# MLP work on VectorE and ScalarE ordered by a list of pieces with needs and due times, and the next layer's first operands made in the last unit

## The chip, the cores and the metric

The kernel runs on one core of a Trainium2 chip as a single launch. The metric is the device time of that launch in microseconds (us). The kernel before takes 2238.01 us (median of three runs, 2237.26 to 2238.69). All arithmetic is in single precision: where TensorE multiplies, each operand is split into a high part (rounded to TensorE's fast format) and a low part (what the rounding left), and three of the four products are summed.

## The reference, cut to what matters

Two layers over 256 tokens of width 2048. Each layer is an attention stage (gated linear attention and stick-breaking attention side by side) and an MLP with a hidden width of 8192:

```python
def hybrid_layer(x, ...):
    h = rms_norm(x, attn_norm)
    proj = h @ w_in
    ...                                  # two groups of heads, each normalised
    x = x + mixed @ w_o
    hm = rms_norm(x, mlp_norm)
    up = square(relu(hm @ w_up))         # 256 x 8192
    return x + up @ w_down
```

The change lies in the MLP and at the seam between the first layer's MLP and the second layer's attention. The attention stage itself is as before.

## The kernel before

**Tiles.** The 256 tokens are two blocks of 128 rows. `x` stays on chip as four tiles `xb[0..3]` of 512 columns. An operand of a product is kept transposed, as eight "pairs" of 256 contraction rows with their high and low parts (class `Operand`).

**Units.** The MLP of a layer is a list of 16 units in the order q = 0 to 3, and in each q: up 0, up 1, down 0, down 1. An up unit makes 1024 of the hidden columns; a down unit adds what q's 2048 hidden rows give to 1024 columns of `x`. A unit goes through eight steps j, each with 256 x 1024 weights (1 MB, one load by the SyncE queue, line 993, five buffers in all). In five steps the product is direct: eight block products. In the three "fast" steps, j = 1, 3 and 5 (line 298), a scheme with seven block products instead of eight (Strassen's, in Winograd's form) is used, for which VectorE first sums weight blocks: `ts` (line 1137), a sum written back into the raw weights, and `t4` (both line 1014 through `add`). A block product is three matmuls of 512 columns (lines 1008, 1010, 1011), so a unit has 5 x 8 x 3 + 3 x 7 x 3 = 183 of them.

**Parts.** Weights are split into high and low in parts of at most 128 x 1024 (`parts`, line 995): ScalarE copies the high part `whi` (line 998), then VectorE subtracts to get `wlo` (line 999). A direct step has two parts (12 matmuls each), a fast one four (6, 3, 6 and 6 matmuls). There are four buffers each of `whi` and `wlo`, so a part can be made when the matmuls of the part four places back are done. The 22 parts of a unit are numbered k = 0 to 21.

**Banks.** The unit sums into eight banks of PSUM named by the scheme's products: banks 5, 7, 1 and 6 are written from k = 4 and 5 on and are final after k = 17; banks 2, 4, 3 and 8 are written from k = 0, 1 on and are final after k = 20 (2 and 4) and k = 21 (3 and 8). When banks are final, VectorE combines them (the "tail" of the unit: `sums`, then the halves `left` and `right`, with `add` on line 1014); a down unit adds them to `xb`, an up unit puts them in `y`, and ScalarE applies the ReLU with the norm's factor (line 1060).

**From up to down.** After an up unit, TensorE transposes each half of `y` (line 1094) behind parts k = 0 and k = 1 of the next unit, into banks 5, 7 and 1, 6; ScalarE squares them (line 1103), and `forms` splits them into high and low (lines 303 and 304) and for fast pairs first makes three sums on VectorE (lines 317 to 320). These four operand pairs are made behind k = 4, 10, 13 and 15 of that unit.

**What sets the order.** In the MLP the order of TensorE, VectorE and ScalarE is the order in which the program is written (`manual_schedule`, line 1210); each engine executes its own list strictly in order. The list is written with a fixed lead: a queue holds four parts whose high and low have been written down, and only then are the oldest part's products written (`LEAD`, `emit`, lines 1192 to 1227), with the tail behind k = 17, 20 and 21. Outside that block a scheduler orders the instructions.

**The seam.** After the last unit the second layer starts with transposes of `xb[0]` and `xb[1]` (16 of them, `norm_operand`, lines 688 and 689; 332 is the transpose, 350 and 352 make the high and the low part), and then the first product with `w_in` (line 425).

Of the kernel before, what the change touches and what calls it, by code (L numbers as in the profile page):

```python
# [35 lines left out]
C_SQ, C_SK, C_SV = 3088, 4112, 5136  # L36


@with_exitstack
def trunk_kernel(  # L40
# [228 lines left out]
    def inv_rms(ss, n, width):  # L269

        v, y, t, t2, rr = stat(n), stat(n), stat(n), stat(n), stat(n)
        nc.vector.tensor_scalar(v, ss, 1.0 / width, EPS, ALU.mult, ALU.add)
        nc.scalar.activation(y, v, AF.Ln)
        nc.scalar.activation(y, y, AF.Exp, scale=-0.5)
        nc.vector.tensor_tensor(t, y, y, ALU.mult)
        nc.vector.scalar_tensor_tensor(t2, t, -0.5, v, ALU.mult, ALU.mult)
        nc.vector.scalar_tensor_tensor(rr, t2, 1.5, y, ALU.add, ALU.mult)
        return rr
# [22 lines left out]
    def split(d, t):  # L301

        nc.scalar.activation(d[:, :, 0, :], t, AF.Copy)  # L303
        return lambda: nc.vector.tensor_tensor(  # L304
            d[:, :, 1, :], t, f32(d[:, :, 0, :]), ALU.subtract
        )

    def forms(op, i, t, tag):

        lows = []
        if fast(i):
            a11, a21, a12, a22 = (t[:, k, r * P : (r + 1) * P] for k in range(2) for r in range(2))
            e = tmp("t2", [P, 3, P], bufs=4)
            d = op.x[i] = tmp(tag, [P, 3, 2, P], F32R, bufs=3)
            nc.vector.tensor_tensor(e[:, 2, :], a21, a11, ALU.subtract)
            nc.vector.tensor_tensor(a21, a21, a22, ALU.subtract)
            nc.vector.tensor_tensor(e[:, 0, :], a11, a21, ALU.subtract)
            nc.vector.tensor_tensor(e[:, 1, :], a12, e[:, 0, :], ALU.subtract)  # L320
            lows.append(split(d, e))
        lows.append(split(op.pair(i), t))
        return lambda: [low() for low in lows]

    def norm_operand(op, n, key, l, sums=False, banks=None):

        for h2 in range(2):
            pt = bank(banks[h2]) if banks else ps_tile()
# [7 lines left out]
            if sums and fast(2 * n + h2):  # L336
                t = tmp("t2", [P, 2, T], bufs=4)
                for j in range(2):
                    nc.scalar.activation(
                        t[:, j, :], pt[:, j * T : (j + 1) * T], AF.Copy,  # L340
                        scale=gain(key, l, 4 * n + 2 * h2 + j),
                    )
                forms(op, 2 * n + h2, t, "sxh")()
                continue
            d = op.pair(2 * n + h2)
            for j in range(2):
                g = gain(key, l, 4 * n + 2 * h2 + j)
                src = pt[:, j * T : (j + 1) * T]
                his.append(
                    nc.scalar.activation(d[:, j, 0, :], src, AF.Copy, scale=g).ins  # L350
                )
                nc.vector.scalar_tensor_tensor(
                    d[:, j, 1, :], src, g, f32(d[:, j, 0, :]), ALU.mult, ALU.subtract
                )

# [296 lines left out]
    for l in range(DEPTH):  # L652
# [30 lines left out]
        else:  # L683
# [4 lines left out]
            for n in range(2):  # L688
                norm_operand(hT, n, "attn", l)
# [280 lines left out]
        up = {}  # L970
        rs = {}
        units = [(q, down, n2) for q in range(4) for down in range(2) for n2 in range(2)]
        raws, banks, ys = {}, {}, {}
        begun = set()
# [10 lines left out]
        def load(x):  # L985
            if x >= 8 * len(units):
                return
            if x % 5 < 2:
                r = tmp("raw2", [P, 2, 1024], bufs=2)
            else:  # L990
                r = wpool.tile([P, 2, 1024], F32, tag="raw", name=nm("raw"))
            raws[x] = r
            nc.sync.dma_start(r, weights(*divmod(x, 8)))

        def parts(r, n=2):
            hi = ppool.tile([P, 2, 512], F32R, tag="whi", name=nm("whi"), bufs=4)
# [278 lines left out]
```

## Time and profile before

| | us |
|---|---|
| median of three runs | 2238.01 |
| the profiled execution, its own time | 2237.89 |
| its span in the profile | 2236.2 |
| MLP of layer 0, first matmul to last | 702.91 |
| MLP of layer 1, first matmul to last | 702.94 |

The profiled execution took 1.7 us more than its span, for what lies before the first and after the last instruction. The MLPs of the two layers are 63% of the span. Times in a view count from the start of the span. "Idle before" stands in brackets with the instruction that ended it. A matmul's record lasts 0.39 us, but a new one can start 0.23 us after the one before, so the records overlap, and a lost fraction of a microsecond does not show as idle time in the sum of busy time; it shows in the starts. In the same way, two VectorE instructions that do not need each other overlap by a little.

### The profile page before, as it was taken

The numbers are of one execution on the slowest core, as the hardware profiler recorded it, in microseconds if no ns is written. First come the engines' busy times: TensorE is split into PE (matmuls) and PEld (weight loads), VectorE is DVE, ScalarE is ACT, GpSimd is POOL, SyncE is SP. The second block draws the span as 40 slices with busy tenths as digits, with TensorE's granted clock in tenths as the row PEclk, the third lists the DMA queues.
The fourth block names the chain that finished last, engine by engine and source line by source line (L and its number), as shares of the span: only waits on it lengthen the run. The fifth ranks groups of instructions, "written<-read, shape, count | busy, mean of one in ns | idle before, by whom it ended". The sixth has DMA issues, their size and how long they took to land.

```text
span 2236.2 us, 27047 instructions
## 1 busy us (share of the span) xinstructions
PE 2201.8 (98%) x10376; PEld 1800.9 (81%) x10376; DVE 1818.7 (81%) x2286; ACT 1246.2 (56%) x1623; POOL 38.0 (2%) x64
## 2 busy tenths in 40 slices
PE   9999999999999999999999999999999999999999
PEld 7988778777887887887888887887778778878877
DVE  5777556789989989989967775667899899899898
ACT  5555355565556466466556553555565655564563
POOL 0020000000000000000000200000000000000000
PEclk9999999999999999999999999999999999999999
DMA  6545446455555555555446544464555555555553
GB/s 227 191 154 167 151 134 243 169 183 194 189 193 183 205 205 175 206 188 188 151 153 201 173 154 150 145 233 172 183 182 216 176 200 189 190 187 199 205 174 138
DMA packets 152549, 408.96 MB, mean 183 GB/s; under 512 B 6650, under 2 KB 31810, under 8 KB 152420
## 3 DMA queue, kind: packets, MB, share of 16 engines
q1 hardware_dynamic: 152420, 407.24, 52.8%
q8 instruction: 81, 1.33, 0.2%
q14 instruction: 48, 0.39, 0.1%
HBM read 405.12 MB, written 2.10 MB: 182 GB/s over the span
## 4 chain that ended last, share of the span: by engine, by line
PE 81%; DVE 15%; issue 2%; ACT 1%; DMA 0%; SPq 0%; POOL 0%; DVEq 0%; ACTq 0%
PE acc L425 9%; PE acc L426 9%; PE acc L427 9%; DVE wlo L999 7%; PE acc L472 3%; PE acc L476 1%; DVE xb L1014 1%; ACT whi L998 1%; DVE t L1014 1%; DVE act L304 1%; DVE ts L1137 1%; DVE act L1014 1%; DVE sx L304 1%; PE ps L895 1%; PE ps L907 1%
## 5 line engine op out<-in xcount | busy, mean ns | idle before, releaser
L999 DVE TENSOR_TENSOR wlo<-raw,whi 128x1024 fp32r<-128x1024 f32 x512 | 610.4, 1220 | 96.4 <-ACT whi L998 92.9
L998 ACT ACTIVATE whi<-raw 128x1024 fp32r<-128x1024 f32 x512 | 528.8, 1054 | 185.2 <-PE acc L427 10.0
L408 DVE TENSOR_TENSOR wlo<-raw,whi 128x1024 fp32r<-128x1024 f32 (+2 forms) x274 | 317.4, 1164 | 195.0 <-ACT whi L406 193.8
L406 ACT ACTIVATE whi<-raw 128x1024 fp32r<-128x1024 f32 (+2 forms) x274 | 273.5, 1004 | 290.9 <-PE acc L427 242.7
L425 PE MATMUL acc<-whi,act 128*128 128x512 f32 (+2 forms) x960 | 368.1, 383 | 1.2 <-ACT act L350 0.9
L426 PE MATMUL acc<-wlo,act 128*128 128x512 f32 (+2 forms) x960 | 362.0, 377 | 0.4 <-DVE wlo L408 0.4
L427 PE MATMUL acc<-whi,act 128*128 128x512 f32 (+2 forms) x960 | 361.6, 377 | 0.0
L998 ACT ACTIVATE whi<-t 128x512 fp32r<-128x512 f32 x96 | 60.8, 633 | 268.7 <-DVE t L1014 143.0
L425 PEld LDWEIGHTS acc<-whi,act 128*128 128x128 f32 x960 | 180.7, 188 | 36.5 <-issue 4.1
L427 PEld LDWEIGHTS acc<-whi,act 128*128 128x128 f32 x960 | 180.5, 188 | 33.9 <-issue 0.7
L426 PEld LDWEIGHTS acc<-wlo,act 128*128 128x128 f32 x960 | 180.8, 188 | 32.0 <-DVE wlo L408 1.2
L999 DVE TENSOR_TENSOR wlo<-ts,whi 128x1024 fp32r<-128x1024 f32 x96 | 117.4, 1223 | 1.4 <-ACT whi L998 1.4
L1137 DVE TENSOR_TENSOR ts<-raw 128x1024 f32<-128x1024 f32 x96 | 116.7, 1216 | 0.0
L998 ACT ACTIVATE whi<-ts 128x1024 fp32r<-128x1024 f32 x96 | 100.4, 1046 | 0.0
L472 PE MATMUL acc<-act,whi 128*128 128x512 f32 x256 | 91.9, 402 | 0.0
L1060 ACT ACTIVATE act<-act,st 128x512 f32<-128x512 f32 x64 | 42.8, 716 | 63.8 <-DVE act L1014 63.8
L476 PE MATMUL acc<-act,wlo 128*128 128x256 f32 x256 | 71.8, 280 | 0.0
L1014 DVE TENSOR_TENSOR raw<-ts,raw 128x512 f32<-128x512 f32 x96 | 66.4, 692 | 3.3
L1014 DVE TENSOR_TENSOR t<-raw 128x512 f32<-128x512 f32 x96 | 66.4, 692 | 3.3
L999 DVE TENSOR_TENSOR wlo<-t,whi 128x512 fp32r<-128x512 f32 x96 | 65.7, 684 | 0.0
L472 PEld LDWEIGHTS acc<-act,whi 128*128 128x128 f32 x256 | 48.1, 188 | 11.1
L303 ACT ACTIVATE sx<-t 128x384 fp32r<-128x384 f32 x24 | 12.6, 526 | 73.9 <-DVE t L320 73.9
(2384 smaller groups left out, 4629.3 us busy)
## 6 DMA issues: line engine op xcount, KB each, us to landing
raw<-in_w_up_dram SPq DMA_DIRECT2D x128, 1024.0 KB, 5.1
raw<-in_w_down_dram SPq DMA_DIRECT2D x128, 1024.0 KB, 5.3
raw<-in_w_in_dram SPq DMA_DIRECT2D x84, 1024.0 KB, 5.1
raw<-in_w_o_dram SPq DMA_DIRECT2D x32, 1024.0 KB, 5.2
raw<-in_w_in_dram SPq DMA_DIRECT2D x14, 512.0 KB, 6.6
raw<-in_w_in_dram SPq DMA_DIRECT2D x8, 544.0 KB, 3.7
out_dram<-xb SPq DMA_DIRECT2D x8, 256.0 KB, 2.0
xb<-in_x_dram SPq DMA_DIRECT2D x3, 512.0 KB, 7.6
```

The costliest lines, as they stand in the source:

```text
L304: return lambda: nc.vector.tensor_tensor(d[:, :, 1, :], t, f32(d[:, :, 0, :]), ALU.subtract)
L406: newest["hi"] = nc.scalar.activation(h, r, AF.Copy).ins
L408: newest["lo"] = nc.vector.tensor_tensor(lo[:, q : q + step, :width], r, f32(h), ALU.subtract).ins
L425: nc.tensor.matmul(o, xh[:, sl], whi[:, j, :width], start=first, stop=False)
L426: nc.tensor.matmul(o, xh[:, sl], wlo[:, j, :width], start=False, stop=False)
L427: st["mm"] = nc.tensor.matmul(o, xl[:, sl], whi[:, j, :width], start=False, stop=last).ins
L472: nc.tensor.matmul(acc[:, f, :], whi[:, j, sl], op.both(k), start=(k == 0), stop=False, skip_group_check=True,)
L476: nc.tensor.matmul(acc[:, f, T:], wlo[:, j, sl], xh, start=False, stop=(k == KT - 1), skip_group_check=True,)
L998: nc.scalar.activation(hi[:, :n], r, AF.Copy)
L999: nc.vector.tensor_tensor(lo[:, :n], r, f32(hi[:, :n]), ALU.subtract)
L1014: nc.vector.tensor_tensor(dst, a, b, ALU.subtract if sub else ALU.add)
L1137: nc.vector.tensor_tensor(t13, ends, b12.unsqueeze(1).to_broadcast([P, 2, 512]), ALU.add)
```

## The change

All MLP work becomes a list of pieces (class `Plan`). A piece has an engine, a length in us written into the program, the pieces that it needs, and a function that writes its instructions. TensorE's and SyncE's pieces keep the order in which they are listed. A piece of VectorE or ScalarE gets a due time: the latest start at which the TensorE work that hangs on it would still start on time, if TensorE never waited. Then `run` plays the list through: whenever VectorE or ScalarE is free, it takes, among the pieces whose needs are met, the one due first. The order found is the order written down, and on the chip each engine follows it as it did the old one. The needs hold the ring of four parts (`whi`, `wlo`), the five weight buffers, the banks and the sums; the high and the low parts keep their order among themselves.

The number and kind of the matmuls, splits, sums and loads are as before. Beside the order, three things differ. `ts` has one buffer and not two. The three sums of a fast pair use a tile `e` of their own (two buffers) and not one of the shared `t2`. And the transposes and splits of `xb[0]` and `xb[1]` for the second layer stand in the last unit of the first layer, behind k = 0 and k = 1, in banks 5, 7 and 1, 6; the second layer's attention starts with its first product. The first unit's `residual(3)` and the transposes of `xb[3]` are pieces of the list too.

```diff
+class Plan:
+    GAP = 0.06
...
+    def run(self):
+        t = 0.0
+        for p in self.pieces:
+            if p.engine == "PE":
+                p.due = t
+                t += p.length
+        for p in reversed(self.pieces):
+            if p.engine != "PE":
+                p.due = min([u.due for u in p.users], default=t) - p.length - p.lag - self.GAP
+        line = {e: [p for p in self.pieces if p.engine == e] for e in ("PE", "SP")}
+        free = dict.fromkeys(("PE", "SP", "DVE", "ACT"), 0.0)
+        left = {p: len(p.deps) for p in self.pieces}
+        at = dict.fromkeys(self.pieces, 0.0)
+        ready = {"DVE": [], "ACT": []}
+        order, events, count = [], [], 0
+        for p in self.pieces:
+            if not p.deps:
+                events.append((0.0, count, p))
+                count += 1
+        came = set()
+        while events:
+            now, _, p = heapq.heappop(events)
+            if p is not None:
+                if p.engine in ready:
+                    heapq.heappush(ready[p.engine], (p.due, count, p))
+                else:
+                    came.add(p)
+                count += 1
+            for e in free:
+                if free[e] > now + 1e-9:
+                    continue
+                if e in ready:
+                    if not ready[e]:
+                        continue
+                    p = heapq.heappop(ready[e])[2]
+                elif line[e] and line[e][0] in came:
+                    p = line[e].pop(0)
+                else:
+                    continue
+                order.append(p)
+                free[e] = now + p.length
+                heapq.heappush(events, (free[e], count, None))
+                count += 1
+                for u in p.users:
+                    at[u] = max(
+                        at[u], free[e] + p.lag + (0.0 if u.engine == e else self.GAP)
+                    )
+                    left[u] -= 1
+                    if not left[u]:
+                        heapq.heappush(events, (at[u], count, u))
+                        count += 1
+        assert len(order) == len(self.pieces)
+        for p in order:
+            if p.fn:
+                p.fn()
+        return max(free.values())
...
+    def operand_parts(op, n, h2, key, l, place):
...
+            e.append(tmp("e", [P, 3, P], bufs=2))
...
             att_psum()
             new_kdz()
             load_gate_up(l)
-            for n in range(2):
-                norm_operand(hT, n, "attn", l)
             uv = unit(
...
+        MM, TR, V2, V1, A2, A1 = 0.227, 0.108, 1.15, 0.61, 1.0, 0.55
+        RING, RAWS = 4, 5
...
+        tail = [add("PE", 12 * MM, None) for _ in range(RING)]
+        for t in tail:
+            whi.append([t])
+            wlo.append([t])
+        x3 = add("DVE", V2, lambda: residual(3, uo), tail)
...
+        def turned(n, h2, m, op, key, ll, deps):
+            turn, high, low, _ = operand_parts(op, n, h2, key, ll, lambda: bank(m))
+            a = add("PE", 8 * TR / 2, turn, deps, free.get(m))
+            b = add("ACT", A1, high, a)
+            c = add("DVE", 1.0, low, b)
+            free[m] = [b, c]
+            return c
...
+            piece = add("SP", 2.9, fn, raws[x - RAWS] if x >= RAWS else [], lag=4.6)
+            raws.append(readers)
+            return (lambda: box[0]), piece, readers
...
+            h = add("ACT", A2 if n == 2 else A1, high, deps, whi[i - RING], last.get("h"))
+            lo = add("DVE", V2 if n == 2 else V1, low, h, wlo[i - RING], last.get("l"))
+            last.update(h=h, l=lo)
+            whi.append([lo])
+            wlo.append([])
+            readers.extend((h, lo))
+            return box, h, lo
...
+                box["13"] = tmp("ts", [P, 2, 512], bufs=1)
...
+            t13 = add("DVE", V2, first, ld, sums13[-1] if sums13 else [])
+            t2 = vector(b12, lambda: box["13"][:, 0, :], lambda: r()[:, 1, 512:], t13)
+            t4 = add("DVE", V1, fourth, t2, sums4[-1] if sums4 else [])
...
+                w = vector(dw, bk(6), dw, c, p[6], op=ALU.subtract)
+                a = vector(x12, dw, x12, w, s[0])
+                v = vector(dw, bk(7), dw, a, p[7])
+                b = vector(x21, x21, dw, v, op=ALU.subtract)
+                d = vector(x22, dw, x22, v, s[1])
+                free.update({5: s[:2], 1: [c, s[2]], 6: [w], 7: [v]})
+                box["s"] = (s[2], b, a, d)
...
+                    free[m] = [add("DVE", V1, fn, p[m], box["s"][2 * c + tt])]
+                    got += free[m]
+                x_done[2 * n2 + c] = got
...
+                    a = add("PE", 4 * TR, turn_one, box["r", h], free[m])
+                    sq = add("ACT", A1, square, a, box.get("sq"))
+                    box["sq"] = sq
+                    free[m] = [sq]
...
+                    e = sq
+                    if fast(pair):
+                        e = add("DVE", 1.25, lambda f=made: f(0), sq)
+                    b = add("ACT", A1 * (2 if fast(pair) else 1), lambda f=made: f(1), e)
+                    done[q, pair] = add(
+                        "DVE", 1.1 if fast(pair) else V1, lambda f=made: f(2), b
                     )
...
+        for u, (q, down, n2) in enumerate(units):
+            tails[u] = (down_tail if down else up_tail)(u)
+            begun, p, k = set(), {}, 0
+            for j in range(8):
+                x = 8 * u + j
+                r, ld, readers = load(x)
+                for (box, h, lo), prods in steps(x, r, ld, readers):
+                    ready = done.get((q, j) if down else ("hm", j))
+                    for m, blocks in prods:
+                        begin, end = m not in begun, j == (7 if m in (2, 4, 3, 8) else lastf)
+                        begun.add(m)
+                        p[m] = add(
+                            "PE", 3 * MM * len(blocks),
+                            lambda a=(m, blocks, box, begin, end): product(*a),
+                            h, lo, ready, free[m] if begin else [],
                         )
+                    whi[-1].append(p[m])
+                    wlo[-1].append(p[m])
+                    if u == 0 and k == 0:
+                        for h2 in range(2):
+                            done["hm", 6 + h2] = turned(
+                                3, h2, (5, 7)[h2], hm, "mlp", l, x3
+                            )
+                        rr, rr_done = norm_last()
+                    if u and k < 2 and not units[u - 1][1]:
+                        tails[u - 1][2](k)
+                    if u + 1 == len(units) and k < 2 and l + 1 < DEPTH:
+                        for h2 in range(2):
+                            turned(
+                                k, h2, ((5, 7), (1, 6))[k][h2], hT, "attn", l + 1, x_done[k]
+                            )
+                    if j == 7:
+                        tails[u][1](k % 2, p)
+                    k += 1
+                if j == lastf:
+                    tails[u][0](p)
+        if l + 1 < DEPTH:
+            sq = [
+                add("ACT", 2 * A1, lambda n=n: norm_squares(n, ssq2), x_done[n])
+                for n in range(4)
+            ]
+            st["rst"], _ = norm_end(sq, ssq2)
         with tc.manual_schedule(engines=MANUAL):
+            plan.run()
...
-        LEAD = 4
-        queue = []
-        tails = {}
-        def emit():
-            u, k, products, w = queue.pop(0)
-            if k == 0:
-                begun.clear()
-                tails[u] = (down_tail if units[u][1] else up_tail)(u), begin(u)
-            products(w)
-            (sums, left, right), extra = tails[u]
-            if k in extra:
-                extra[k]()
-            for at, fn in ((17, sums), (20, left), (21, right)):
-                if k == at:
-                    fn()
-            for x in range(4):
-                load(x)
-            for x in range(8 * len(units)):
-                load(x + 4)
-                u, j = divmod(x, 8)
-                if j == 0:
-                    count = 0
-                for i, (prepare, products) in enumerate(steps(x)):
-                    if j == 1 and i == 0:
-                        while queue[0][0] < u:
-                            emit()
-                    queue.append((u, count, products, prepare()))
-                    count += 1
-                    if x == 0 and i == 1:
-                        residual(3, uo)
-                    if len(queue) >= LEAD and (u or count >= LEAD):
-                        emit()
-            while queue:
-                emit()
-            if l + 1 < DEPTH:
-                for n in range(4):
-                    norm_squares(n, ssq2)
-                st["rst"] = norm_finish(ssq2)
```

455 lines of the change are left out of this document (255 added, 200 removed).

## Prediction

> **What bounds the kernel now.** I read the page first, then the busy time of each engine in windows that begin and end with a unit's first matmul, then the timeline around the units that are too long.
>
> ```profile
> span 2236.2 us, 27047 instructions
> PE 2201.8 (98%) x10376; PEld 1800.9 (81%) x10376; DVE 1818.7 (81%) x2286; ACT 1246.2 (56%) x1623; POOL 38.0 (2%) x64
> PE 81%; DVE 15%; issue 2%; ACT 1%; DMA 0%; SPq 0%; POOL 0%; DVEq 0%; ACTq 0%
> ```
>
> TensorE is busy nearly all the time, yet 15% of the chain that ended last runs through VectorE. What TensorE loses is seen only in the length of the units. First five units of layer 0, then both MLPs whole (columns: length; busy time and instructions of TensorE, its weight loads, VectorE, ScalarE, GpSimd; granted clock, DMA share, GB/s):
>
> ```profile
> 417.53:462.12 44.59, 43.31 (x192) 35.02 (x191) 39.61 (x48) 25.33 (x35) 0.00 (x0) 1.00 0.52 189
> 462.12:508.63 46.51, 44.77 (x201) 35.51 (x199) 40.97 (x52) 27.18 (x36) 0.00 (x0) 1.00 0.46 158
> 508.63:553.97 45.34, 44.22 (x200) 35.70 (x200) 42.80 (x53) 29.15 (x37) 0.00 (x0) 1.00 0.53 186
> 553.97:595.57 41.60, 41.60 (x184) 34.42 (x184) 39.17 (x44) 21.67 (x23) 0.00 (x0) 1.00 0.57 206
> 595.57:637.05 41.48, 41.48 (x185) 34.35 (x183) 37.61 (x41) 22.42 (x25) 0.00 (x0) 1.00 0.61 224
> ...
> 417.53:1120.44 702.91, 690.45 (x3066) 560.53 (x3064) 644.16 (x757) 408.19 (x499) 1.69 (x2) 1.00 0.53 187
> 1529.27:2232.21 702.94, 690.35 (x3065) 560.43 (x3063) 643.11 (x755) 401.55 (x483) 0.00 (x0) 1.00 0.53 186
> ```
>
> The same 183 matmuls take 41.48 us in the fifth unit (an up unit behind a down unit), 41.60 in the fourth, but 46.51 and 45.34 in the second and third, which also hold the transposes, and 44.59 in the first. The clock is full and DMA is at half its capacity throughout. A matmul starts every 0.227 us (last four below: 0.68 us for three steps), and 183 of them make 41.5: the fifth unit has no loss at all.
>
> What do the transposes cost by themselves?
>
> ```profile
> 464.62 0.39 PE L1011 MATMUL m__754_4002<-whi,act 128*128 128x512 f32 x1
> 464.85 0.60 PE L1094 MATMUL m__755_4009<-ident,act 128*128 128x128 f32 x4
> 465.28 0.60 PE L1094 MATMUL m__756_4014<-ident,act 128*128 128x128 f32 x4
> 465.64 0.48 PE L1008 MATMUL m__759_4023<-whi,act 128*128 128x512 f32 x1
> 465.95 0.40 PE L1010 MATMUL m__759_4023<-wlo,act 128*128 128x512 f32 x1
> ```
>
> From 464.62 to 465.95 are 1.33 us with two matmul steps in them: 0.88 for one half. A unit behind an up unit has two halves, 1.75, so its floor is 43.23; the first unit has one (`xb[3]`), floor 42.36. Lost are: second unit 3.28, third 2.11, fourth 0.12, first 2.23. If this comes again in every q, a layer loses 2.23 + 4 x (3.28 + 2.11 + 0.12) = 24.3 us; it does, for 702.91 less 16 x 41.48 and 17 halves of 0.88 is 24.3 too. Both layers: 48.5.
>
> Where do the 3.28 come from? Timeline of the second unit, VectorE, ScalarE and TensorE around the longest gap:
>
> ```profile
> 495.08 0.28 DVE L317 TENSOR_TENSOR t<-act 128x128 f32<-128x128 f32 x1
> 496.05 0.29 DVE L320 TENSOR_TENSOR t<-act,t 128x128 f32<-128x128 f32 x1
> 498.40 1.22 DVE L999 TENSOR_TENSOR wlo<-raw,whi 128x1024 fp32r<-128x1024 f32 x1 [2.06 <-ACT whi L998]
> 496.38 0.53 ACT L303 ACTIVATE sx<-t 128x384 fp32r<-128x384 f32 x1 [3.92 <-DVE t L320]
> 497.33 1.99 ACT L998 ACTIVATE whi<-raw 128x1024 fp32r<-128x1024 f32 x2
> 497.62 0.39 PE L1011 MATMUL m__754_4002<-whi,act 128*128 128x512 f32 x1
> 498.42 0.50 PE L1008 MATMUL m__759_4023<-whi,act 128*128 128x512 f32 x1 [0.42 <-ACT whi L998]
> 499.68 0.50 PE L1010 MATMUL m__759_4023<-wlo,act 128*128 128x512 f32 x1 [0.76 <-DVE wlo L999]
> ```
>
> ScalarE stood idle for 3.92 us behind an `sx` copy that waited for VectorE's sums, with the next `whi`, due at once, queued behind it; then VectorE stood idle 2.06 us for that `whi`; TensorE, with no part left, lost 0.57 and 1.03 us. The work was there; the written order put pieces not yet needed ahead of one that was. Over the program:
>
> ```profile
> ACT whi L998 <- DVE t L1014: 143.0, 53, 7.2
> DVE wlo L999 <- ACT whi L998: 94.3, 102, 2.1
> ACT sx L303 <- DVE t L320: 73.9, 24, 3.9
> ```
>
> **The change part by part.**
>
> *The order, second unit.* No instruction is added; the question is whether VectorE has room. It needs 40.97 us of busy time in a floor of 43.23 and has 5.5 idle today. In the fourth unit it ran 39.17 in 41.60 (idle 5.8%) at a loss of 0.12, in a fixed order. At the same idle share the second unit takes 40.97/0.942 = 43.5: gain 3.0 of 3.28. Four per layer: 12.0. Bounds: half of it (1.6 each) where new cross waits appear, 3.28 at best.
>
> *Third unit.* Here VectorE needs 42.80 of 43.23, 99%. At the fourth unit's idle share this would be 45.4, no gain; with perfect order 2.11. Against the first speaks that the tail's sums need not end with the unit: banks 5, 7, 1 and 6 are wanted only at the next unit's k = 4, and that unit has 2.4 us of VectorE idle. I take two thirds, 1.4; four per layer: 5.6.
>
> *First unit.* Its loss begins with `residual(3)`:
>
> ```profile
> 417.74 1.23 DVE L953 TENSOR_TENSOR xb<-acc,xb 128x1024 f32<-128x1024 f32 x1 [3.12 <-PE acc L427]
> 418.88 1.22 DVE L1137 TENSOR_TENSOR ts<-raw 128x1024 f32<-128x1024 f32 x1
> ```
>
> VectorE waited 3.12 us for the last product of the stage before, with the first `ts` behind it. The list lets `ts` go ahead; 1.1 us of the queue is off, and the splits of `xb[3]`, now due by banks 5 and 7, share the rest. I take 1.7 of 2.23; bounds 0 and 2.23.
>
> Per layer 12.0 + 5.6 + 1.7 = 19.3; two layers 38.6.
>
> *Loads.* 128 a layer as before on SyncE's queue, each behind the four to seven readers of the buffer five loads back, as now; cost nothing, hidden by DMA at 0.46 to 0.61 of its time. If a load were late by 1 us it would first hit `ts`, then k = 3 of a fast step.
>
> *One `ts` buffer.* The next `ts` sum now waits until both readers of the last are done. Between one fast step's third part and the next's second, TensorE has 6 + 6 + 12 + 12 + 6 matmuls, 9.5 us. In it VectorE must do four `wlo` of 1.14, then the chain `ts`, sum, `t4`, split. The rows' durations for one chain and for instructions that need each other:
>
> ```profile
> 545.76 0.68 DVE L1014 TENSOR_TENSOR xb<-m__863_4477,xb 128x512 f32<-128x512 f32 x1
> 546.36 0.68 DVE L1014 TENSOR_TENSOR t<-m__864_4481,t 128x512 f32<-128x512 f32 x1
> 547.07 0.69 DVE L1014 TENSOR_TENSOR xb<-t,xb 128x512 f32<-128x512 f32 x1
> 549.73 3.49 DVE L999 TENSOR_TENSOR wlo<-raw,whi 128x1024 fp32r<-128x1024 f32 x3
> ```
>
> Three `wlo` take 3.49, so (3.49 - 1.22)/2 = 1.14 a piece; the 512-wide sums 0.60, or 0.71 behind one they need. Four `wlo` and the chain: 4.5 + 1.2 + 0.7 + 0.7 + 0.7 = 7.8 of 9.5. Room of 1.7: nothing, unless a fast pair's `forms` fall in the same stretch (four sums, 1.3 us from 495.08 on, and two splits of at most 0.6 each: up to 2.5).
>
> An instruction that needs nothing of the one before thus starts 0.085 us before that one's record ends. [...]
>
> *The seam.*
>
> ```profile
> 1119.53 0.39 PE L1011 MATMUL m__1814_8970<-whi,act 128*128 128x512 f32 x1
> ...
> 1120.21 0.39 PE L1011 MATMUL m__1814_8970<-whi,act 128*128 128x512 f32 x1
> 1120.44 0.60 PE L332 MATMUL ps<-ident,xb 128*128 128x128 f32 x4
> 1122.13 1.54 PE L332 MATMUL ps<-ident,xb 128*128 128x128 f32 x12 [1.09 <-DVE xb L1014]
> 1123.42 0.48 PE L425 MATMUL acc<-whi,act 128*128 128x512 f32 x1
> ```
>
> From the last MLP matmul to the first of attention are 3.21 us. Taken off: all but one step, 2.98. Put back: two halves of transposes in the last unit, 1.75. Rest 1.23. But eight splits each on ScalarE and VectorE move with them:
>
> ```profile
> L352 DVE SCALAR_TENSOR_TENSOR act<-ps,gcol_a,act 128x256 fp32r<-128x256 f32 x32 | 14.3, 479 | 2.9 <-ACT act L350 2.7
> ```
>
> On VectorE 14.3/32 x 8 = 3.6 us, which bring the last unit, by the fourth's 39.17, to 42.8 of 43.23, as tight as the third; with that unit's remainder of 0.7 the seam gives 0.5. The transposes' new wait is met: `xb[0]` is final in the unit before, and `xb[1]` two sums (0.68 each) after its last product, while its transposes stand behind two parts, 5.4 us. What stands behind them on TensorE, k = 1 and 2, would wait if not; k = 4 and 5 wait for the splits to free the banks, two to four parts later. Bounds -1.2 (the wait for the last `xb` sum moves to attention's first product) and +1.2.
>
> Sum: 38.6 + 0.5 = 39.1 off the profiled execution's own 2237.89 (its median is 0.1 higher, which is no difference here): 2198.8, forecast **2199**. All floors met: 2237.9 - 48.5 - 1.2 = 2188.
>
> **The rivals.** *A, half the gain.* VectorE becomes the bound in second and third units: the order is computed from fixed lengths and executed in order, so that a piece that is late by a few tenths holds those behind it. The second unit gains 1.6, the third and the first nothing: 8 x 1.6 = 13, 2225; with half of the third's and the first's loss besides, 8 x 2.7 + 2.2 = 24, 2214. For it: 99% in the third unit. Against: 94% ran freely in the fourth.
>
> *B, slower.* The single `ts` buffer: `forms` fall into the 9.5 us stretch, and `t4` is late at k = 3 of fast steps. Their 2.5 us less the 1.7 of room are at most 0.8 a fast step. If the order makes all 96 fast steps of the program pay, the units that are clean today too, it decides from 0.5 us a step on (48 against the 49 won); at 0.6 it is 2237.9 - 49 + 58 = 2247. Against: clean units have no `forms`.
>
> *C, nothing changes.* The same waits come back in another place, 2234 to 2242. Against: the new list knows the pieces that blocked.
>
> *D, no overlap on VectorE.* If each instruction held VectorE for its whole record, as those that need each other do, the second unit would need up to 40.97 + 52 x 0.085 = 45.4 us and gain 1.1, the third nothing: 8 x 1.1 + 2 x 1.7 + 0.5 = 12.7, 2225. Against: 1.14 for 1.22, and the third unit's 53 instructions would need 47.3 us and take 45.34. [...]
>
> **How the numbers follow.** Forecast (2188 to 2209) 0.68; A 0.22; B 0.04; C 0.04; D 0.02. Faster by over 0.2% (what a measurement of this kernel can tell from no change, 4.5 us): forecast, A, D and a quarter of C, 0.93; same 0.02 (half of C); slower 0.05 (B and the rest of C). The range: lower end 2188, no unit can go under its floor; upper end into A until two tenths are out, 2214.
>
> **What would show it.** Right: second units at 43.2 to 43.8, third at 43.2 to 44.2, first at 42.4 to 43.2; "ACT sx from DVE t" and "ACT whi from DVE t" mostly gone; the seam's first product 0.3 to 0.5 us behind the last MLP matmul. Wrong: units at 41.5 today that grow past 42, waits of TensorE on `wlo` from `t4` or `ts`, an idle VectorE in second units again, or a wait for `xb` ahead of attention's first product.

## The result and the profile after

The changed kernel takes 2199.91 us (median of four runs, 2199.17 to 2201.5), the kernel before, on the same chip, 2237.98: a ratio of 0.9831, 95% interval 0.9814 to 0.9848, or 38.1 us less. 39.1 were forecast off the profiled execution. The interval lies below 1, so it is faster, by 1.7%. The profiled execution of after took 2201.5 us, its span 2199.8; between the two profiled executions the difference is 36.4.

The page of after: span, busy time of the engines, and the shares of the chain that ended last.

```profile
span 2199.8 us, 27163 instructions
PE 2187.7 (99%) x10376; PEld 1806.0 (82%) x10376; DVE 1790.0 (81%) x2286; ACT 1259.7 (57%) x1623; POOL 38.0 (2%) x64
PE 90%; DVE 7%; issue 1%; ACT 1%; DMA 0%; SPq 0%; POOL 0%; ACTq 0%
```

The count of instructions on TensorE, VectorE, ScalarE and GpSimd is the same. VectorE's share of the chain has halved, from 15 to 7%, and its busy time has fallen by 28.7 us, which nothing in the prediction had.

The same windows as before, first matmul of a unit to first matmul of the next: first five units of layer 0, its last unit, and the two MLPs.

```profile
418.26:461.26 43.00, 42.68 (x192) 35.11 (x191) 39.29 (x50) 26.33 (x36) 0.00 (x0) 1.00 0.57 188
461.26:505.38 44.12, 43.70 (x200) 35.86 (x199) 41.04 (x54) 29.37 (x38) 0.00 (x0) 1.00 0.58 191
505.38:548.68 43.30, 43.30 (x201) 36.02 (x199) 39.60 (x49) 27.60 (x34) 0.00 (x0) 1.00 0.57 192
548.68:590.40 41.72, 41.72 (x185) 34.28 (x183) 38.21 (x44) 22.00 (x23) 0.00 (x0) 1.00 0.61 202
590.40:632.08 41.68, 41.68 (x185) 34.28 (x183) 38.20 (x44) 23.48 (x26) 0.00 (x0) 1.00 0.63 205
1061.22:1105.53 44.31, 43.90 (x200) 35.70 (x199) 41.27 (x52) 27.33 (x41) 0.30 (x1) 1.00 0.42 133
418.26:1105.53 687.27, 684.95 (x3081) 563.94 (x3080) 632.38 (x764) 419.20 (x507) 1.69 (x2) 1.00 0.58 192
1511.25:2195.81 684.56, 682.71 (x3065) 562.33 (x3063) 627.76 (x754) 409.35 (x483) 0.00 (x0) 1.00 0.58 191
```

The first unit went from 44.59 to 43.00, the second from 46.51 to 44.12, the third from 45.34 to 43.30, its floor; the fourth and fifth grew by 0.12 and 0.20. Layer 1's MLP is 18.4 shorter. Layer 0's is 15.6 shorter although its last unit now holds the transposes for the next layer. From the last MLP matmul of layer 0 to the first of layer 1's MLP (1105.30 to 1511.25) are 405.95 us, against 409.06 (1120.21 to 1529.27): 3.1 less. The MLP of layer 0 begins 0.7 later, which is put down here to the attention stage before it, not to the change (in the runs below, with that stage the same, the MLP begins anywhere from 415.8 to 418.3). 18.4 + 15.6 + 3.1 - 0.7 = 36.4.

The groups of waits of after (total us, count, longest):

```profile
DVE wlo L1179 <- ACT whi L1175: 106.1, 92, 1.5
ACT whi L1175 <- DVE t L1098: 60.7, 35, 5.1
ACT act L1344 <- DVE act L1098: 25.4, 32, 1.1
```

ScalarE's wait for `t` is 60.7 instead of 143.0, and that of the `sx` copies, 73.9 before, is gone.

What is left in a second unit, in the timeline of after:

```profile
480.26 2.01 ACT L1175 ACTIVATE whi<-raw 128x1024 fp32r<-128x1024 f32 x2 [0.24 <-PE m__764_4027 L1260]
480.82 1.22 DVE L1179 TENSOR_TENSOR wlo<-raw,whi 128x1024 fp32r<-128x1024 f32 x1
481.95 1.21 DVE L1098 TENSOR_TENSOR ts<-raw 128x1024 f32<-128x1024 f32 x1
483.09 1.21 DVE L1179 TENSOR_TENSOR wlo<-raw,whi 128x1024 fp32r<-128x1024 f32 x1
483.55 0.39 PE L1258 MATMUL m__756_3993<-whi,act 128*128 128x512 f32 x1
...
484.36 0.50 PE L1259 MATMUL m__756_3993<-wlo,act 128*128 128x512 f32 x1 [0.42 <-DVE wlo L1179]
```

The second of the two `whi` ends at 482.27, 0.3 us after VectorE took up a `ts` that nobody needed yet; its `wlo`, the urgent one, starts at 483.09. TensorE's two starts are 0.81 apart instead of 0.23. The list takes what is due first among the pieces that are ready, and it takes something whenever anything is ready.

The seam in the timeline of after:

```profile
1105.30 0.39 PE L1260 MATMUL m__1825_8996<-whi,act 128*128 128x512 f32 x1
1105.53 0.39 PE L549 MATMUL acc<-whi,act 128*128 128x512 f32 x1
```

The next layer's first product follows one matmul step behind.

### The profile page after: what moved, and what is told of

Same layout as the page of the kernel before. It is cut to its first block, busy times and chain, and to the rows that moved or that the text cites. A ratio compares the mean times of both kernels' runs of the same rounds, so it can differ in the third digit from the quotient of the medians.

```text
span 2199.8 us, 27163 instructions
## 1 busy us (share of the span) xinstructions
PE 2187.7 (99%) x10376; PEld 1806.0 (82%) x10376; DVE 1790.0 (81%) x2286; ACT 1259.7 (57%) x1623; POOL 38.0 (2%) x64
## 4 chain that ended last, share of the span: by engine, by line
PE 90%; DVE 7%; issue 1%; ACT 1%; DMA 0%; SPq 0%; POOL 0%; ACTq 0%
PE acc L549 9%; PE acc L551 9%; PE acc L550 9%; DVE wlo L1179 3%; PE acc L596 3%; PE acc L600 1%; DVE ts L1098 1%; DVE act L426 1%; PE ps L1017 1%; PE ps L1029 1%; ACT whi L1175 1%; PE ps L441 0%; PE ps L976 0%; PE ps L712 0%; DVE sx L426 0%
## 5 line engine op out<-in xcount | busy, mean ns | idle before, releaser
L1179 DVE TENSOR_TENSOR wlo<-raw,whi 128x1024 fp32r<-128x1024 f32 x512 | 618.5, 1217 | 56.8 <-ACT whi L1175 52.9
L1175 ACT ACTIVATE whi<-t 128x512 fp32r<-128x512 f32 x96 | 60.6, 631 | 122.2 <-DVE t L1098 60.7
L600 PEld LDWEIGHTS acc<-act,wlo 128*128 128x128 f32 x256 | 48.4, 189 | 0.1
```

The lines of the kernel that those rows point to most:

```text
L600: nc.tensor.matmul(acc[:, f, T:], wlo[:, j, sl], xh, start=False, stop=(k == KT - 1), skip_group_check=True,)
L1175: nc.scalar.activation(box["h"][:, :n], src(), AF.Copy)
L1179: nc.vector.tensor_tensor(box["l"][:, :n], src(), f32(box["h"][:, :n]), ALU.subtract)
```

## Experiments

The theory to be tested: the time was lost to the order and not to VectorE's capacity; the due times won it back; what is left comes from starting an unneeded piece just ahead of an urgent one. Against it stand rival A (VectorE itself is full, or an order from fixed lengths is held up by pieces that are late) and rival B (the single `ts`).

**1. Without due times: the piece that is ready first goes first.**

```diff
-                    heapq.heappush(ready[p.engine], (p.due, count, p))
+                    heapq.heappush(ready[p.engine], (0.0, count, p))
```

> The changed kernel, but a free VectorE or ScalarE takes the piece whose needs were met first; the due times are not used, all else is as changed. Theory (the due times carry the gain: urgent parts go ahead of sums that can wait): 10 to 30 us of the 38 come back, 2210 to 2230, with waits of TensorE on wlo in all kinds of units. Rival (what cost time was only that an engine stood behind a piece whose needs were not met; any order that takes ready pieces alone does away with it): 2198 to 2204.

Measured: 2250.78 us, ratio to before 1.0057 (1.0042 to 1.0072), slower than the hand-written order and beyond the 2210 to 2230 expected. Fourth unit, and a row of TensorE's timeline in it:

```profile
551.24:594.43 43.19, 41.84 (x184) 34.20 (x183) 38.41 (x44) 22.12 (x23) 0.00 (x0) 1.00 0.58 197
```
```profile
554.11 0.50 PE L1258 MATMUL m__920_4754<-whi,act 128*128 128x512 f32 x1 [1.35 <-DVE xb L1098]
```

VectorE does the same work (38.41 us; 38.21 in after), but a `xb` sum that frees a bank comes late, and a unit that was clean loses 1.6. Everything else of the change is in this kernel too (the pieces, the single `ts`, the tile `e`, the moved seam), so none of that makes it faster by itself: the due times carry more than the whole gain.

A small part of the 12.8 us is the clock. In one unit of each layer TensorE stands idle for 2.21 us behind a `wlo`, and then the granted clock is half for 3.41 us (the first of the two):

```profile
828.97 0.80 PE L1259 MATMUL m__1352_6792<-wlo,act 128*128 128x512 f32 x1 [2.21 <-DVE wlo L1179]
828.93:832.34 3.41, 3.37 (x8) 2.70 (x9) 3.41 (x5) 0.00 (x0) 0.00 (x0) 0.50 0.11 17
```

Those two units take 47.3 us where the same units elsewhere in the run take 45.8, so 3.0 us in all.

**2. Due times, and a look ahead.** While the list is played through, a ready piece is passed over if its length would make a more urgent one late whose start is already known.

```diff
-                    p = heapq.heappop(ready[e])[2]
+                    pick = None
+                    for item in sorted(ready[e]):
+                        c = item[2]
+                        if not any(
+                            s.due < c.due and now + c.length > max(at[s], s.due + late)
+                            for s in soon[e]
+                        ):
+                            pick = item
+                            break
+                    if pick is None:
+                        continue
```

(`soon` holds the pieces of an engine whose needs have all been started, `late` is how far TensorE is behind its due times.)

> The changed kernel, but a free engine leaves a ready piece, and waits if it must, where that piece would make a more urgent one late whose start is already known. Theory (what is left in second units, 0.87 us, and in fourth and fifth, 0.2 each, comes from a ts or weight sum begun some tenths of a us before a wlo that was due could start): second units 43.3 to 43.6, the others within 0.1 of their floors, 2188 to 2194 in all. Rival (VectorE is simply full in second units): they stay at 44.0, 2198 to 2202, or grow because VectorE now waits.

Measured: 2189.58 us, ratio 0.9782 (0.9768 to 0.9797), faster than both kernels. Second, third and fourth unit:

```profile
459.02:502.36 43.34, 43.34 (x201) 35.93 (x199) 41.11 (x54) 29.41 (x38) 0.00 (x0) 1.00 0.60 194
502.36:545.65 43.29, 43.29 (x201) 36.02 (x199) 39.59 (x49) 27.59 (x34) 0.00 (x0) 1.00 0.58 191
545.65:587.16 41.51, 41.51 (x185) 34.35 (x183) 38.22 (x44) 22.00 (x23) 0.00 (x0) 1.00 0.60 203
```

With the same work on VectorE (41.11; 41.04 in after) the second unit falls from 44.12 to 43.34. All units but layer 0's last are within 0.15 us of the floors that the prediction took from the transposes' rows. Layer 0's last unit, which holds the moved transposes, takes 43.77. So the rest of after's loss, in the second units as in the fourth and fifth, was the early start of unneeded pieces.

**3. The seam alone, put back**, once in after and once in the version with the look ahead.

```diff
             load_gate_up(l)
+            for n in range(2):
+                norm_operand(hT, n, "attn", l)
...
-                    if u + 1 == len(units) and k < 2 and l + 1 < DEPTH:
-                        for h2 in range(2):
-                            turned(
-                                k, h2, ((5, 7), (1, 6))[k][h2], hT, "attn", l + 1, x_done[k]
-                            )
```

> The changed kernel, but the transposes and splits of xb[0] and xb[1] are back at the start of the second layer. Theory (the seam is worth about 0.5 us, as predicted: 3.0 off the gap, 2.6 on the last unit): 2200 to 2201.5, the gap from the last MLP matmul to attention's first product near 3.2 again, the last unit at 41.7. Rival (the moved splits cost the last unit nothing that counts, so the seam is worth 1.2 or more): 2201.2 to 2203; or it is worth less than nothing: below 2199.5.

> The kernel that looks ahead (e2), with the seam as before the change. Theory (with the last unit at its floor the seam is worth 2.98 less 1.75 or a little less): 1.0 to 1.5 us more than e2, 2190.5 to 2191.2; last unit 41.5, gap 3.2. Rival (the last unit was never the place; the seam's worth is the same 0.5 or less): 2189.2 to 2190.2.

Measured: 2201.27 us, ratio 0.9837 (0.9822 to 0.9851), and 2191.85, ratio 0.9791 (0.9777 to 0.9806): 1.4 and 2.3 above the versions with the moved seam, but the intervals overlap, and the second was measured on another chip than its version with the moved seam (the kernel before takes 0.55 longer there). The traces tell more. From the last MLP matmul to layer 1's MLP are 410.21 us instead of 405.95 with the seam back in after, and the last unit is 41.7 instead of 44.31: the move is worth 4.26 - 2.6 = 1.7 there. With the look ahead it is 1.5 by the same reckoning (409.79 - 406.04 outside the MLP, 43.77 - 41.51 in the last unit). So in after the traces give the rival's 1.2 or more and not the theory's 0.5, though not for the rival's reason: the moved splits do cost the last unit 2.6, and what differs is the old seam. Its gap to attention's first product is 2.84 us, where 3.2 was expected. With the look ahead the traces give the 1.0 to 1.5 of the theory, though the time itself, 2191.85, lies above its 2191.2. One row of the first of the two shows what the old seam has beside that gap:

```profile
1106.65 0.50 PE L551 MATMUL acc<-whi,act 128*128 128x512 f32 x1 [0.79 <-DVE act L457]
```

Attention's third product waits for a split. Before the change that wait was not there. It is one part of why this stretch is 1.15 us longer than before's 409.06; the rest was not traced. So the move is worth 0.5 against before's own seam and more against the old seam behind the new order.

**4. The old order with one cause removed**: in the kernel before, the four sums of a fast pair (three in a tile of their own, one in place) are written two parts earlier, and nothing else is changed.

```diff
+        def early(u, i):
+            ys[u]["e", i] = form_sums(ys[u]["t", i // 2][:, i % 2])
...
+                if fast(4 * units[p][2] + i):
+                    work[k - 2] = lambda i=i, f=work.get(k - 2): (f and f(), early(p, i))
```

> The kernel before with one edit: the four sums of a fast pair (lines 317 to 320) are written two parts ahead of the copy that needs them. Theory (ScalarE stood behind that copy with the next whi queued behind it): the 74 us of ScalarE's waits for these sums vanish, second units fall from 46.5 to 44.5 to 45.5, 2222 to 2230 in all. Rival (VectorE's load in these units sets the time): the wait goes elsewhere, 2236 to 2240.

Measured: 2222.75 us, ratio 0.993 (0.9914 to 0.9947). Second units went from 46.5 to 44.9, third from 45.3 to 45.1. Waits of this kernel:

```profile
ACT whi L1010 <- DVE t L1026: 176.4, 52, 7.2
...
ACT sx L303 <- DVE t L314: 10.3, 24, 0.9
```

The `sx` wait, 73.9 before, is 10.3: the stall that the prediction read off at 496.38 was what it seemed, and one hand-made move wins 15 of the 38 us. The other large wait grows from 143.0 to 176.4, and the time falls all the same.

**5. Two `ts` buffers in after.** (The sums of a fast pair go to the shared `t2` again, for room.)

```diff
-                box["13"] = tmp("ts", [P, 2, 512], bufs=1)
+                box["13"] = tmp("ts", [P, 2, 512], bufs=2)
...
-            t13 = add("DVE", V2, first, ld, sums13[-1] if sums13 else [])
+            t13 = add("DVE", V2, first, ld, sums13[-2] if len(sums13) > 1 else [])
```

> The changed kernel with two buffers for ts, as before the change (the pair's sums e go back to the shared tile, for the room). Theory (one buffer costs nothing; with two, an engine that takes any ready piece begins a ts sum still earlier, ahead of parts that are due): not faster, 2200 to 2226, with more waits of TensorE on wlo. Rival (the prediction's B in small: the single buffer is what is left in the units): 2193 to 2198.

Measured: 2220.53 us, ratio 0.9921 (0.9906 to 0.9936): 20 slower than with one buffer. Second and fourth unit:

```profile
460.73:504.61 43.88, 43.59 (x201) 35.90 (x199) 40.94 (x54) 29.33 (x38) 0.00 (x0) 1.00 0.58 192
547.90:591.21 43.31, 42.38 (x184) 34.14 (x183) 38.13 (x44) 21.98 (x23) 0.00 (x0) 1.00 0.57 195
```

The fourth and fifth units go from 41.7 to 43.3. The units that hold the fast pairs' sums did not grow (second 44.12 to 43.88, third 43.3 in both), so it is the second `ts` that costs and not the shared `t2`. VectorE in the fourth:

```profile
557.61 1.22 DVE L1098 TENSOR_TENSOR ts<-raw 128x1024 f32<-128x1024 f32 x1
558.75 1.22 DVE L1179 TENSOR_TENSOR wlo<-raw,whi 128x1024 fp32r<-128x1024 f32 x1
...
560.02 0.50 PE L1259 MATMUL m__917_4739<-wlo,act 128*128 128x512 f32 x1 [0.62 <-DVE wlo L1179]
```

TensorE waits at 560.02 for the `wlo` that stood behind a `ts`. Rival B falls, and turns round: going by this row, the single buffer had kept the list from beginning sums too soon. Whether the look ahead would make two buffers harmless was not tried.

**6. More work on VectorE.** The version with the look ahead, and in each unit four more 128 x 512 sums whose results are used by nothing.

```diff
+                if j in (0, 2, 4, 6):
+                    def pad():
+                        w = tmp("t2", [P, 512], bufs=4)
+                        combine(w, xb[0][:, 0, :], xb[0][:, 1, :])
+                    readers.append(add("DVE", V1, pad, ld))
```

> The kernel that looks ahead (e2), with four sums more on VectorE in every unit (128x512, 0.6 us each, results not used): 43.5 us of VectorE in second units, 42.0 in third, 40.6 in fourth and fifth. Theory (VectorE's busy time costs nothing until it comes to the unit's floor, and the neighbours take what is over): units grow by 0.3 at most, 2189 to 2196. Rival (at 95% and over, each VectorE instruction costs its time, as the prediction held for third units at 99%): second and third units grow by 1 to 2.4 each, 2203 to 2230.

Measured: 2192.02 us, ratio 0.9794 (0.9778 to 0.9811). 128 sums, 77 us at 0.60 each, cost 2.4 by the medians, which the intervals do not tell from nothing. The fullest unit:

```profile
842.96:886.26 43.30, 43.30 (x200) 36.03 (x199) 43.03 (x56) 27.63 (x34) 0.00 (x0) 1.00 0.60 196
```

VectorE is busy for 43.03 of 43.30 us, and the unit is within 0.1 of its floor of 43.23. The first half of rival A, VectorE full at 41 to 43 us of a unit, falls.

**7. Wrong lengths.** The program's lengths are near what the rows show: 1.15 for a `wlo` (pitch 1.14), 0.61 for a 512-wide sum (0.60), 1.0 for a `whi` of two (2.01/2). What if they weren't? In after all four lengths of VectorE and ScalarE by 0.8, then VectorE's alone; with the look ahead all four by 0.8, and by 1.2.

```diff
-        MM, TR, V2, V1, A2, A1 = 0.227, 0.108, 1.15, 0.61, 1.0, 0.55
+        MM, TR, V2, V1, A2, A1 = 0.227, 0.108, 0.92, 0.488, 0.8, 0.44
```

> The changed kernel (no look ahead) with the four lengths of VectorE's and ScalarE's pieces written 20% too short. Theory (order matters, lengths only roughly: due times move by tenths and the engines take care of the rest): 2193 to 2206. Rival A of the prediction (executed in order, pieces that are late by tenths hold those behind them): 2212 or more.

> The changed kernel with the lengths of VectorE's pieces alone written 20% too short (e8 had ScalarE's too). Theory (the play-through then sees VectorE with a quarter of its time to spare and starts sums that can wait in front of parts that on the chip come late): most of e8's 70 us, 2240 to 2275. Rival (ScalarE's lengths did it: the play-through sees whi ready before it is, and VectorE stands behind its wlo): 2198 to 2215.

> The kernel that looks ahead (e2) with all four lengths 20% too short, as e8. Theory (looking ahead takes away the harm, as less urgent sums are not begun in front of a part that is due): 2190 to 2205. Rival (the look ahead reckons with the same wrong lengths, so it does not see the collision): 2230 to 2270, like e8.

> The kernel that looks ahead (e2) with all four lengths 20% too long: VectorE then has more work than there is time in the play-through. Theory (too long is safer than too short: everything is late there, so the order is by due time throughout, and on the chip the engines catch up): 2189 to 2200. Rival (any error of 20% spoils the order, as in e8): 2220 to 2270.

Measured: 2269.92 (ratio 1.014, 1.0125 to 1.0155), 2255.64 (1.0079, 1.0064 to 1.0094), 2269.39 (1.014, 1.0125 to 1.0155) and 2219.87 (0.9918, 0.9901 to 0.9935). Lengths that are 20% short lose 70 us, almost twice what the change wins; VectorE's alone lose 56 of them; the look ahead, which reckons with the same lengths, does not help: the rival holds there. The first of these kernels, VectorE and a matmul that waits:

```profile
740.68 1.22 DVE L1098 TENSOR_TENSOR ts<-raw 128x1024 f32<-128x1024 f32 x1
...
741.94 0.69 DVE L1098 TENSOR_TENSOR raw<-ts,raw 128x512 f32<-128x512 f32 x1
...
742.67 0.69 DVE L1098 TENSOR_TENSOR t<-raw 128x512 f32<-128x512 f32 x1
...
743.28 3.49 DVE L1179 TENSOR_TENSOR wlo<-raw,whi 128x1024 fp32r<-128x1024 f32 x3
...
744.55 0.50 PE L1259 MATMUL m__1236_6219<-wlo,act 128*128 128x512 f32 x1 [0.70 <-DVE wlo L1179]
```

The three sums take 2.60 us (740.68 to 743.28) and were put down at 1.90, so the `wlo` behind them starts 0.70 later than by the written lengths, and TensorE stands idle waiting for it. This is the second half of rival A, and it is real when the lengths are 20% short.

Lengths 20% long were expected to be harmless, 2189 to 2200, and cost 30 us. Third unit of that run, with the second ahead of it:

```profile
459.04:502.32 43.28, 43.28 (x201) 36.02 (x199) 37.38 (x42) 27.19 (x33) 0.00 (x0) 1.00 0.59 195
502.32:548.02 45.70, 44.33 (x200) 35.88 (x199) 45.00 (x63) 29.05 (x38) 0.00 (x0) 1.00 0.56 184
```

By these lengths VectorE can't keep up (41.1 x 1.2 = 49 us of a 43 us unit), and 12 instructions fewer than with the right lengths stand in the second unit (42 for 54) and 14 more in the third (63 for 49). That one then needs 45.00 us, more than its floor: here VectorE is the bound, because of where the order puts its work.

**8. Sums that need each other kept together.** The version with the look ahead, `ts`, sum and `t4` of a fast step as one piece.

```diff
+                combine(b12(), box["13"][:, 0, :], r()[:, 1, 512:])
+                fourth()
...
-            t13 = add("DVE", V2, first, ld, sums13[-1] if sums13 else [])
-            t2 = vector(b12, lambda: box["13"][:, 0, :], lambda: r()[:, 1, 512:], t13)
-            t4 = add("DVE", V1, fourth, t2, sums4[-1] if sums4 else [])
+            t13 = t2 = t4 = add(
+                "DVE", V2 + 2 * V1, first, ld, sums13[-1] if sums13 else [],
+                sums4[-1] if sums4 else [],
+            )
```

> The kernel that looks ahead (e2) with the three weight sums of a fast step (ts, the sum into raw, t4) as one piece, so that they stand directly behind one another as before the change. Theory (an instruction that needs the one before starts about 0.1 us later than one that does not, and it is the mixing that took 3.5 us per four units off VectorE's busy time): VectorE's busy time grows by 0.5 to 0.8 a unit; the units stay at their floors, 2189 to 2192. Rival (the busy time fell for another reason): VectorE's busy time stays within 0.2 a unit.

Measured: 2201.49 us, ratio 0.9835 (0.982 to 0.985): 12 slower than with three pieces. The timeline of a fourth unit:

```profile
561.96 1.22 DVE L1118 TENSOR_TENSOR ts<-raw 128x1024 f32<-128x1024 f32 x1
...
563.22 0.69 DVE L1118 TENSOR_TENSOR raw<-ts,raw 128x512 f32<-128x512 f32 x1
...
563.94 0.69 DVE L1118 TENSOR_TENSOR t<-raw 128x512 f32<-128x512 f32 x1
564.55 3.49 DVE L1199 TENSOR_TENSOR wlo<-raw,whi 128x1024 fp32r<-128x1024 f32 x3
...
565.82 0.50 PE L1282 MATMUL m__935_4812<-wlo,act 128*128 128x512 f32 x1 [0.30 <-DVE wlo L1199]
```

VectorE's busy time rose by 0.5 us a unit as expected (1806.6 in all, 1790.9 without the joining). The time was not expected to follow: in the units that were clean a `wlo` comes late (42.2 us instead of 41.5). A piece of 2.6 us that can't be interrupted is one reason; another is that its length is written as 2.37, which is 0.23 short. The two were not told apart.

## Why the prediction was right, and where not

**The forecast.** 2199.0 was predicted and 2199.91 measured. The mechanism held; that the total came out so close is in part luck. By the profiled executions 36.4 of the 39.1 came: 18.4 and 18.2 from the two MLPs (the second figure with the 2.6 of the moved transposes taken out) for 19.3 each, 0.5 from the seam as forecast, and 0.7 lost before the MLP. Within the MLP two terms missed in opposite directions: over both layers the second units fell short by 8 x 0.6 = 4.8 us, and the third units won 8 x 0.64 = 5.1 more than forecast.

**Loss by order.** Held. Writing four sums earlier (4) wins 15 us in the old order; with the look ahead (2) the same instructions take 2189.58 us, where the prediction had 2188 for all floors met.

**Second unit, "the same idle share ... gain 3.0".** Mis-sized: 2.4. The step took VectorE's room as the limit. It was not: at the same VectorE time the look ahead gives 43.34, and in (6) a unit with 42.46 us on VectorE takes 43.28. What was short is the choice of the piece, a `ts` 0.3 us too soon.

**Third unit, "99% ... I take two thirds, 1.4".** Mis-sized the other way: 2.04, all there was but 0.07. Busy time of 99% does not cost a third (43.03 of 43.30 in (6) costs next to nothing), and it is not 99% any more: 42.80 became 39.60. Four 512-wide instructions fewer stand in the unit, which makes 2.8 us of it. One sum of the tail runs on into the next unit, which was the argument for the 1.4; the other three, a sum of the tail before and two weight sums, are done earlier. The other 0.4 is that neighbours on VectorE overlap more, which was not seen.

**First unit.** 1.7 forecast, 1.6 measured, in the way described, by VectorE's timeline of after: `ts` runs while `residual(3)` still waits.

```profile
415.26 1.22 DVE L1098 TENSOR_TENSOR ts<-raw 128x1024 f32<-128x1024 f32 x1
418.46 1.22 DVE L1075 TENSOR_TENSOR xb<-acc,xb 128x1024 f32<-128x1024 f32 x1 [1.99 <-PE acc L551]
```

**Fourth and fifth units.** The sum has no term for them; they lost 0.12 and 0.20, about 1.1 a layer (four fourth units, three fifth). Same cause as in the second unit: with the look ahead they take 41.51 and 41.50. Per layer: 1.6 + 4 x (2.4 + 2.04 - 0.12) - 3 x 0.20 = 18.3 of the measured 18.4; 19.3 was forecast.

**One `ts` buffer.** "Nothing" held, and by (5) more than that: a second one costs 20 us.

**The seam.** 0.5 forecast: 3.1 won outside the MLP, 2.6 paid in the last unit (44.31 over 41.72), 0.5 left. The last unit's remainder, taken as 0.7, is 44.31 - 43.23 = 1.1, although VectorE is busy for 41.27 us in it and not for the 42.8 reckoned; as in the second unit, VectorE's room was not the limit.

**The rivals.** A's time is wrong, and its first reason too; its second is real at lengths 20% short. B, C and D fall. For D: the `ts` at 481.95 has a record of 1.21 us and the `wlo` behind it, which doesn't need it, starts 1.14 later. A sum that reads the one before does start later, 1.26 behind a `ts` in (7). The Trainium skill ("VectorE: DVE Perf Modes", section "The DRAIN you can't avoid") has the next instruction wait until the pipe is empty, but adds that one that is not held starts earlier. The starts 1.14 apart agree with that addition; what makes an instruction held was not tried here.

**The signs named in advance.** Third and first unit and the seam fell where they should, the seam's first product at 0.23 even under the 0.3 to 0.5 given. The second unit did not (44.12, not 43.2 to 43.8), and of the waits only `sx` is gone; `whi` behind `t` went to less than half. Of the signs against, one came: waits on a `wlo` behind `ts`.

**Open.** How much error in the lengths can be borne short of the 20% that were tried (as written they fit single instructions, but a chain of three sums, put down at 2.37, takes 2.60); whether the look ahead would make a second `ts` harmless; and why the old seam is slower behind the new order.

## What to carry to other kernels

A loss on a busy TensorE that comes from the order of two helper engines can be counted from unit lengths against a clean unit, and an order by due times wins it back; what decides is that the urgent piece goes first and that nothing long is begun just ahead of it, so the play-through should look ahead (10.3 us here). Such an order is only as good as its lengths: measure them as pitches in the trace, independent and dependent ones apart, and take them neither 20% short nor long. A busy share of 99% on a helper engine is no bound by itself, and a further buffer or a larger piece can cost time where it lets unneeded work start ahead of needed work.

## What was not expected of the hardware

VectorE's busy time fell by 28.7 us (1818.7 to 1790.0) with 2286 instructions in both. A sum that reads the one before starts 1.26 us behind a 1024-wide one and 0.73 behind a 512-wide one (the chain in (7), 740.68 to 741.94 to 742.67), an independent one 1.14 behind a 1024-wide one (481.95 to 483.09), and the due times happen to place other pieces between the sums of a chain. Joining the weight sums of the 96 fast steps again (8) brought 15.7 us back, 0.16 a step; VectorE's busy time is in these lines, first with the look ahead, then joined:

```profile
PE 2179.8 (100%) x10376; PEld 1806.5 (83%) x10376; DVE 1790.9 (82%) x2286; ACT 1259.4 (58%) x1623; POOL 37.9 (2%) x64
PE 2187.5 (99%) x10376; PEld 1803.6 (82%) x10376; DVE 1806.6 (82%) x2286; ACT 1255.7 (57%) x1623; POOL 38.0 (2%) x64
```

The whole traces of before and after bear this out. VectorE's records add up to 1924.6 us before and 1920.7 after; but the time in which one starts before the last has ended grew from 105.9 to 130.8 us. So 24.9 of the 28.7 us are overlap. That the part beyond the weight sums comes from the chains of the tails and of the fast pairs is likely, and was not tried.

TensorE's clock was not expected either: behind a wait of 2.21 us TensorE was granted half its clock for 3.41 us, and matmuls started 0.43 apart instead of 0.23 (the second view of (1)).
